# Scores of window attention: stacked 128-deep products of one head, or three 64-deep products of two heads

## The chip, the cores and the metric

The kernel runs on one core of a Trainium2 chip. The metric is device time in microseconds (us), the median of the runs. PE is the matrix engine (its weight loads are listed as PEld), DVE the vector engine, ACT the scalar engine, POOL the general engine (GpSimd), SP the queue that issues transfers.

## What is computed

One layer of a mixer for 2048 latent tokens (a grid of 32 rows by 64 columns) and 128 context tokens, 1024 channels wide, all in float32 at the inputs and outputs. One input projection feeds three branches; the change touches the third alone, attention with 8 heads of 64 channels.

```python
h = layernorm(x) * (1 + scale) + shift
xa, ba, ca, ga, u, v, gb, q, k, vv, gc = split(h @ w_in)
# latent tokens: each block of 8 x 16 queries sees its 2-D window and all 128 context keys
s_loc = q . k_window * 64**-0.5 + rel_bias      # window keys outside 8 x 16 are masked
s_ctx = q . cache_k * 64**-0.5
p = softmax(concat[s_loc, s_ctx]);  out = p_loc @ v_window + p_ctx @ cache_v
# context tokens: dense attention among the 128 context tokens
y = concat[conv branch, gMLP branch, out * silu(gc)] @ w_out
x_new = layernorm(ALPHA * x + gate * y) * ln_g + ln_b
```

## The kernel before

Activations lie with channels in the partitions, split into a float16 high and low part (`h_hi`, `h_lo`), and so are the weights. After a stage for the gMLP branch and the values, a list of jobs is worked off: for each head pair `hp` (0 to 3) a job `q`, a job `k` and a job `gc`, with jobs of the convolution (`xa`, `ca`, `ba`, `ga`) between them. A job makes 128 output channels for the five token tiles of `TILES` (four of 512, one of 128), 24 matmuls a tile, in `proj` (L505). The last stage is the output projection.

For each head pair, the `q` job (L1186) rounds the projected queries into `QS`: for head h, float16 high parts in one half of the partitions and the rest (low parts) in the other half, by two ACT and two DVE instructions a tile on 64 partitions each. The `k` job (L1195) writes the keys' high parts `KH` and low parts `KL`, each head in its own half, and SP then copies each half of `KH` and `KL` into the other half of the head's plane (L1223 to L1227). So a matmul over 128 partitions gives high times key plus low times key at once, and the scores of a head are two products: with `KH` and with `KL`.

Attention of a head pair is 17 units: 16 blocks of 128 queries (window keys: 352 columns in the first four units, 480 in the next eight, 384 in the last four, and 128 context keys each) and the 128 context queries. `scores(u, h)` (L993) issues the four matmuls of one head of a unit (two for unit 16) into a tile `s` of PSUM, of which there are two buffers, and the start of the softmax: DVE adds the bias table `TB` and takes the row's maximum (L1020, "reduce" below; it frees `s`, and the bias table for POOL to build the next one, L979) and scales the maximum (L1025). The rest of the softmax follows as five events: `expo` (L1029, ACT), `norm` (L1032 and L1033, DVE), `high` (L1036, ACT), `low` (L1039, DVE) and `turn` (L1045, a transposing transfer on SP). `values` (L1053) multiplies the turned probabilities `ptr` with the values, two heads in the two column halves of the array, and DVE writes the gated result (L1072, `yc`).

What stands where in each engine's row is decided when the program is built. A planned clock `now` advances by the columns of each projection matmul over 2.4 GHz (`tick`), by the score columns in `scores` and by 240 ns a block of keys in `values`; events are posted with a due time on that clock and come out between two projection matmuls when they are due. The table `T` holds the times: a unit of a head pair every `pace` (6.0, 6.0, 4.9 and 4.7 us), the second head half a pace after the first, and the five events 0.7, 0.7, 2.1, 2.75 and 3.7 us after the scores of their head. Each engine then works strictly through its row and waits where an operand is missing. The next `q` job drains what is left of the attention of the pair before (`finish`, L1243).

Of the kernel before, what the change touches and what calls it, by code (L numbers as in the profile page):

```python
# [22 lines left out]
P = 128  # L23
D = 1024
KB = 8
LAT = 2048
CTX = 128
TOK = LAT + CTX
# [57 lines left out]
    a_half=0.5,  # L86
    pace=(6000.0, 6000.0, 4900.0, 4700.0),
# [48 lines left out]
def hybrid_step(ctx: ExitStack, tc: tile.TileContext, x_prompt, x_sample, cache_k, cache_v, c, c_ctx,  # L136
# [781 lines left out]
    QS = ap.tile([P, 2, TOK], F16, name="QS")  # L918
    KH = ap.tile([P, 2, TOK + CTX], F16, name="KH")
    KL = ap.tile([P, 2, TOK + CTX], F16, name="KL")  # L920
# [61 lines left out]
    class Attn:  # L982
        def __init__(self, hp, pace):
            self.hp = hp
            self.ys = None
            self.ts = {}
            for u in range(17):
                if u:
                    post(T['a_start'][hp] + (u - T['a_tab']) * pace, lambda u=u: make_tables(u), ("at", hp, u))
                for h in range(2):  # L990
                    post(T['a_start'][hp] + (u + T['a_half'] * h) * pace, lambda u=u, h=h: self.scores(u, h), ("as", hp, u))

        def scores(self, u, h):  # L993
            i = 2 * u + h
            drain(("a", self.hp, i - T['a_guard']), ("at", self.hp, u))
            tg = ("a", self.hp, i)
            sm = ap.tile([P, 4], F32, name="sm", bufs=8)
            s = aps.tile([P, 2, 512], F32, name="s", tag="s", bufs=2)
            if u < 16:
                rb, j = UNITS[u]  # L1000
                nr = RB_NROW[rb]
                n = 32 * nr
                q = QS[:, h, u * P:(u + 1) * P]
                for e, kk in enumerate((KH, KL)):
                    PE.matmul(out=s[:, 0, 384:512], lhsT=q, rhs=kk[:, h, TOK:TOK + CTX], start=(e == 0), stop=(e == 1))
                for e, kk in enumerate((KH, KL)):
                    win = kk[:, h, RB_ROW0[rb] * 64:(RB_ROW0[rb] + nr) * 64].rearrange("p (r c) -> p r c", c=64)
                    PE.matmul(out=s[:, 1, 0:n], lhsT=q, rhs=win[:, :, COL0[j]:COL0[j] + 32], start=(e == 0), stop=(e == 1))  # L1008
            else:
                n = 0  # L1010
                q = QS[:, h, LAT:TOK]
                for e, kk in enumerate((KH, KL)):
                    PE.matmul(out=s[:, 0, 384:512], lhsT=q, rhs=kk[:, h, LAT:TOK], start=(e == 0), stop=(e == 1))
            now[0] += 2 * (P + n) / 2.4
# [113 lines left out]
    while cidx < len(jobs):  # L1128
# [37 lines left out]
        for ti, (t0, n) in enumerate(TILES):  # L1166
# [19 lines left out]
            if kind == "q":  # L1186
                for u in range(4 * ti, min(4 * ti + 4, 17)):
                    drain(("as", idx - 1, u))
                S.activation(out=QS[0:64, 0, t0:t0 + n], in_=ps[0:64], func=AF.Copy, scale=cq[0:64])
                S.activation(out=QS[64:128, 1, t0:t0 + n], in_=ps[64:128], func=AF.Copy, scale=cq[64:128])  # L1190
                V.scalar_tensor_tensor(out=QS[64:128, 0, t0:t0 + n], in0=ps[0:64], scalar=cq[0:64],
                                       in1=QS[0:64, 0, t0:t0 + n], op0=ALU.mult, op1=ALU.subtract)
                V.scalar_tensor_tensor(out=QS[0:64, 1, t0:t0 + n], in0=ps[64:128], scalar=cq[64:128],
                                       in1=QS[64:128, 1, t0:t0 + n], op0=ALU.mult, op1=ALU.subtract)
            elif kind == "k":  # L1195
                for h in range(2):
                    a = slice(64 * h, 64 * h + 64)
                    S.activation(out=KH[a, h, t0:t0 + n], in_=ps[a], func=AF.Copy, scale=ckk[a])  # L1198
                    V.scalar_tensor_tensor(out=KL[a, h, t0:t0 + n], in0=ps[a], scalar=ckk[a], in1=KH[a, h, t0:t0 + n],  # L1199
                                           op0=ALU.mult, op1=ALU.subtract)  # L1200
                rng = {1: (0, 1024), 3: (1024, 2048)}.get(ti)
                if ti == 0:
                    cps = aps.tile([P, P], F32, name="cps", tag="o")
                    PE.transpose(cps, ckt, ident)
                    for h in range(2):
                        a = slice(64 * h, 64 * h + 64)
                        S.activation(out=KH[a, h, TOK:], in_=cps[a], func=AF.Copy, scale=s_k[a])
                        V.scalar_tensor_tensor(out=KL[a, h, TOK:], in0=cps[a], scalar=s_k[a], in1=KH[a, h, TOK:],
                                               op0=ALU.mult, op1=ALU.subtract)
                if ti == 4:  # L1210
                    rng = (2048, TOK + CTX)
# [155 lines left out]
```

## Time and profile before

| | before |
|---|---|
| runs | 1193.34, 1196.65, 1197.59 us (median 1196.65) |
| profiled execution | 1199.64 us, span 1197.7 us |
| PE busy | 1070.1 us (89%) |
| DVE busy | 846.7 us (71%) |
| ACT busy | 444.8 us (37%) |
| POOL busy | 346.2 us (29%) |
| granted clock of PE | 0.963 of 2.4 GHz over the span |
| attention of head pair 0, 1, 2, 3 | from 423, 565, 712, 840 to some 533, 678, 806, 940 us |

A busy time is a sum over the span, so the shares say which engine could be the bound, and the windows of the four attention stretches say in which of them it is. In a timeline the first column is the start, the second the duration; matmuls overlap in the array, so what one costs there is the distance between two starts. A wait belongs to the instruction that waited, and the arrow names what ended it. Between the four stretches lie the `k` jobs (some 30 us each), in which no attention runs.

### The profile page before, as it was taken

What the parts mean: (1) busy time and instruction counts of PE and PEld (TensorE: products, weight loads), DVE (VectorE), ACT (ScalarE), POOL (GpSimd) and SP (SyncE); (2) the same over time, 40 slices, a digit from 0 to 9 for tenths busy, and PEclk for the clock granted to TensorE, in tenths of its full rate; (3) what the DMA queues carried; (4) which work ended last, traced back from release to release, by engine and by line L of the source; (5) the groups of instructions that cost most, each with busy time, mean ns of one, the idle gap of its engine ahead of it and who ended that gap; (6) DMA issues with size and microseconds to landing.
All of it is one profiled execution on the core that took longest, in us unless ns stands there. A gap on an engine that the chain in (4) does not pass through costs nothing. (4 is left out here: it accounts for less than half of the span.)

```text
span 1197.7 us, 21038 instructions
## 1 busy us (share of the span) xinstructions
PE 1070.1 (89%) x8044; PEld 684.0 (57%) x8044; DVE 846.7 (71%) x2073; ACT 444.8 (37%) x756; POOL 346.2 (29%) x346
## 2 busy tenths in 40 slices
PE   5378989889986999999999999989988999888885
PEld 1267875468773555554545445545545477776674
DVE  1778875665662379863898549983899558877877
ACT  0233322122322356543655436663666321112111
POOL 0135765200002032101662022300325405434434
PEclk9589999889997999999999999999999999999998
DMA  9703201348969237755566646767466663343341
GB/s 346 238 5 113 85 9 56 130 153 292 295 206 245 52 80 134 143 112 122 101 143 130 144 103 131 150 121 157 94 139 117 203 200 108 124 139 105 111 136 53
DMA packets 254356, 165.50 MB, mean 138 GB/s; under 512 B 163600, under 2 KB 224808, under 8 KB 254256
## 3 DMA queue, kind: packets, MB, share of 16 engines
q1 hardware_dynamic: 254256, 164.16, 52.7%
q8 instruction: 63, 1.03, 0.4%
q14 instruction: 37, 0.30, 0.1%
HBM read 88.06 MB, written 36.21 MB: 104 GB/s over the span
## 5 line engine op out<-in xcount | busy, mean ns | idle before, releaser
L508 PE MATMUL pj<-h_hi,wring 128*128 128x512 f16 (+1 forms) x1280 | 335.9, 349 | 9.6 <-DMA wring<-wj_d 9.6
L508 PEld LDWEIGHTS <-wring 128*128 128x128 f16 x2400 | 212.9, 99 | 224.6 <-DMA wring<-wj_d 9.7
L508 PE MATMUL pj<-h_lo,wring 128*128 128x512 f16 (+1 forms) x640 | 217.7, 349 | 0.0
L1296 PE MATMUL ps<-wo,yh 128*128 128x512 f32 (+1 forms) x840 | 193.6, 390 | 20.9 <-DVE yh L1106 20.9
L1296 PEld LDWEIGHTS ps<-wo,yh 128*128 128x128 f32 x840 | 154.0, 189 | 60.4 <-DVE yh L1106 27.0
L1039 DVE SCALAR_TENSOR_TENSOR PH<-pt,sm,PH 128x608 f16<-128x608 f32 (+3 forms) x136 | 155.6, 1144 | 2.6 <-ACT PH L1036 2.4
L979 POOL TENSOR_TENSOR TB<-raw,msk 128x480 f32<-128x480 f32 (+2 forms) x96 | 96.1, 1010 | 186.9 <-DVE sm L1020 186.8
L1036 ACT ACTIVATE PH<-pt,sm 128x608 f16<-128x608 f32 (+3 forms) x136 | 99.9, 734 | 95.1 <-ACT pt L1029 63.3
L1029 ACT ACTIVATE pt<-pt,sm,scal 128x608 f32<-128x608 f32 (+2 forms) x128 | 108.3, 846 | 56.9 <-DVE sm L1025 53.3
L1020 DVE CUSTOM_DVE_ANT_0 pt<-s,TB 128x608 f32<-128x608 f32 (+2 forms) x128 | 93.3, 729 | 10.5 <-PE s L1008 9.7
L518 PE MATMUL vvps<-wV,h_hi 128*128 128x256 f16 x544 | 92.9, 275 | 3.7 <-DVE vt L900 3.6
L518 PEld LDWEIGHTS <-h_hi 128*128 128x128 f16 x816 | 80.8, 100 | 20.3 <-issue 9.3
L508 PE MATMUL p<-h_hi,wring 128*128 128x512 f16 (+1 forms) x320 | 87.2, 358 | 2.9 <-DVE th L525 2.9
L1320 ACT ACTIVATE r<-r,omv 128x1024 f32<-128x1024 f32 x16 | 19.9, 1245 | 177.2 <-issue 141.1
L508 PEld LDWEIGHTS <-wB 128*128 128x128 f16 x768 | 65.9, 102 | 25.6 <-issue 3.4
L1321 POOL TENSOR_TENSOR r<-r,gam 128x1024 f32<-128x1024 f32 x16 | 38.2, 2387 | 128.0 <-ACT r L1320 128.0
L518 PE MATMUL vvps<-wV,h_lo 128*128 128x256 f16 x272 | 74.8, 275 | 0.0
L508 PE MATMUL ups<-h_hi,wB 128*128 128x128 f16 (+2 forms) x448 | 72.9, 274 | 0.0
L963 POOL TENSOR_SCALAR raw<-raw,scal 128x528 f32<-128x528 f32 x8 | 5.5, 704 | 219.8 <-DVE scal L189 165.4
L1106 DVE TENSOR_TENSOR yh<-yf,yh 128x1024 fp32r<-128x1024 f32 x17 | 41.0, 2410 | 35.2 <-ACT yh L1105 35.2
L1199 DVE SCALAR_TENSOR_TENSOR KL<-pj,scal,KH 64x512 f16<-64x512 f32 (+1 forms) x40 | 26.8, 669 | 54.1 <-ACT KH L1198 53.9
L456 POOL TENSOR_TENSOR h_lo<-hf,h_hi 128x512 f16<-128x512 f32 x34 | 39.9, 1179 | 85.0 <-DMA wstage<-in_w_in_dram 37.8
(212 smaller groups left out, 1715.4 us busy)
## 6 DMA issues: line engine op xcount, KB each, us to landing
wa<-in_w_ada_dram SPq DMA_DIRECT2D x24, 512.0 KB, 7.2
wraw<-in_w_in_dram SPq DMA_DIRECT2D x20, 512.0 KB, 5.7
wj_d<-wsp SPq DMA_DIRECT2D x40, 256.0 KB, 6.1
wring<-wj_d SPq DMA_DIRECT2D x20, 512.0 KB, 6.0
yf<-y_d SPq DMA_DIRECT2D x17, 512.0 KB, 5.6
xt<-in_x_sample_dram SPq DMA_DIRECT2D x16, 512.0 KB, 4.7
VW<-v_d SPq DMA_DIRECT2D x64, 128.0 KB, 5.1
xr<-in_x_sample_dram SPq DMA_DIRECT2D x16, 512.0 KB, 4.1
```

What stands on the lines that cost most here:

```text
L456: G.tensor_tensor(out=h_lo[:, k0:k0 + g, t0:t0 + n], in0=hv, in1=hi, op=ALU.subtract)
L508: PE.matmul(out=ps, lhsT=w(a, k) if callable(w) else w[:, a, k, :], rhs=mov(b, k), start=(k == 0 and i == 0), stop=(k == KB - 1 and i == 2))
L518: PE.matmul(out=ps, lhsT=a[:, k, i * P:(i + 1) * P], rhs=w[:, b, k, :], start=(k == 0 and q == 0), stop=(k == KB - 1 and q == 2))
L979: G.tensor_tensor(out=TB[:, tslot(u) + h, P:P + n], in0=raws[h][:, off:off + n], in1=msk[:, mo:mo + n], op=ALU.add)
L1020: V.tensor_tensor_reduce(out=pt[:, :w], in0=src, in1=TB[:, tslot(u) + h, 0:w], op0=ALU.add, op1=ALU.max, scale=1.0, scalar=-3e38, accum_ou ...
L1029: S.activation(out=pt[:, :w], in_=src, func=AF.Exp, bias=sm[:, 1:2], scale=st_["isig"], accum_out=sm[:, 2:3])
L1036: S.activation(out=pb[:, 0:w], in_=pt[:, :w], func=AF.Copy, scale=sm[:, 3:4])
L1039: V.scalar_tensor_tensor(out=pb[:, wp:wp + w], in0=pt[:, :w], scalar=sm[:, 3:4], in1=pb[:, 0:w], op0=ALU.mult, op1=ALU.subtract)
L1106: V.tensor_tensor(out=yh[:, 1], in0=yf, in1=yh[:, 0].bitcast(F32), op=ALU.subtract)
L1199: V.scalar_tensor_tensor(out=KL[a, h, t0:t0 + n], in0=ps[a], scalar=ckk[a], in1=KH[a, h, t0:t0 + n], op0=ALU.mult, op1=ALU.subtract)
L1296: PE.matmul(out=ps, lhsT=yh[:, a, k, :], rhs=wo[:, b, k, f0:f1], start=(k == 0 and q == 0), stop=(k == KB - 1 and q == 2))
L1321: G.tensor_tensor(out=r, in0=r, in1=gam, op=ALU.mult)
```

## The change

`QH`, `QL`, `KH` and `KL` hold the queries' and keys' high and low parts with the channels where the projection leaves them: head 0 in partitions 0 to 63, head 1 in 64 to 127. One ACT and one DVE instruction on 128 partitions write a tile, and the 24 copies by SP are gone. The scores of a head are now three products over 64 partitions (high with high, low with high, high with low; the fourth, low with low, is left out), 12 matmuls a unit in which the two heads alternate. `scores(u)` issues both heads of a unit; the softmax's start is in a function of its own, `soft(u, h)`, which is posted for the second head half a pace later, as before. The planned clock advances by 3 times the columns of a unit instead of 4 times. Nothing in `T` is changed.

```diff
             for u in range(17):
                 if u:
                     post(T['a_start'][hp] + (u - T['a_tab']) * pace, lambda u=u: make_tables(u), ("at", hp, u))
+                post(T['a_start'][hp] + u * pace, lambda u=u: self.scores(u), ("as", hp, u))
                 for h in range(2):
-                    post(T['a_start'][hp] + (u + T['a_half'] * h) * pace, lambda u=u, h=h: self.scores(u, h), ("as", hp, u))
+                    post(T['a_start'][hp] + (u + T['a_half'] * h) * pace, lambda u=u, h=h: self.soft(u, h), ("as", hp, u))
...
-        def scores(self, u, h):
-            i = 2 * u + h
-            drain(("a", self.hp, i - T['a_guard']), ("at", self.hp, u))
+        def scores(self, u):
+            drain(("a", self.hp, 2 * u - T['a_guard']), ("at", self.hp, u))
...
+            s = [aps.tile([P, 2, 512], F32, name="s", tag="s", bufs=2) for h in range(2)]
+            pairs = ((QH, KH), (QL, KH), (QH, KL))
+            for e, (q, kk) in enumerate(pairs):
+                for h in range(2):
+                    a = slice(64 * h, 64 * h + 64)
+                    k0 = TOK if u < 16 else LAT
+                    PE.matmul(out=s[h][:, 0, 384:512], lhsT=q[a, t0:t0 + P], rhs=kk[a, k0:k0 + CTX], start=(e == 0), stop=(e == 2))
...
-            now[0] += 2 * (P + n) / 2.4
+            now[0] += 3 * (P + n) / 2.4
+            self.ss[u] = s
+
+        def soft(self, u, h):
+            i = 2 * u + h
+            tg = ("a", self.hp, i)
+            sm = ap.tile([P, 4], F32, name="sm", bufs=8)
+            s = self.ss[u][h]
...
-                S.activation(out=QS[0:64, 0, t0:t0 + n], in_=ps[0:64], func=AF.Copy, scale=cq[0:64])
-                S.activation(out=QS[64:128, 1, t0:t0 + n], in_=ps[64:128], func=AF.Copy, scale=cq[64:128])
-                V.scalar_tensor_tensor(out=QS[64:128, 0, t0:t0 + n], in0=ps[0:64], scalar=cq[0:64],
...
+                S.activation(out=QH[:, t0:t0 + n], in_=ps, func=AF.Copy, scale=cq)
+                V.scalar_tensor_tensor(out=QL[:, t0:t0 + n], in0=ps, scalar=cq, in1=QH[:, t0:t0 + n],
+                                       op0=ALU.mult, op1=ALU.subtract)
...
-                if rng:
-                    r = slice(*rng)
-                    for kk in (KH, KL):
-                        SP.dma_start(out=kk[64:128, 0, r], in_=kk[0:64, 0, r])
-                        SP.dma_start(out=kk[0:64, 1, r], in_=kk[64:128, 1, r])
```

In PE's row, a unit of 480 window columns of head pair 0. Before, one head (the other stands half a pace later, behind more projection matmuls):

```order
L1005 LDWEIGHTS QS_4034
L1005 MATMUL s_4917<-KH_4035,QS_4034 128x128
L1005 LDWEIGHTS QS_4034
L1005 MATMUL s_4917<-KL_4036,QS_4034 128x128
L1008 LDWEIGHTS QS_4034
L1008 MATMUL s_4917<-KH_4035,QS_4034 128x480
L1008 LDWEIGHTS QS_4034
L1008 MATMUL s_4917<-KL_4036,QS_4034 128x480
L508 LDWEIGHTS wring_4130
```

Now the second half of the unit's 12 matmuls (both heads, `s_4915` and `s_4916`):

```order
L1016 LDWEIGHTS QH_4034
L1016 MATMUL s_4915<-KH_4036,QH_4034 128x480
L1016 LDWEIGHTS QH_4034
L1016 MATMUL s_4916<-KH_4036,QH_4034 128x480
L1016 LDWEIGHTS QL_4035
L1016 MATMUL s_4915<-KH_4036,QL_4035 128x480
L1016 LDWEIGHTS QL_4035
L1016 MATMUL s_4916<-KH_4036,QL_4035 128x480
L1016 LDWEIGHTS QH_4034
L1016 MATMUL s_4915<-KL_4037,QH_4034 128x480
L1016 LDWEIGHTS QH_4034
L1016 MATMUL s_4916<-KL_4037,QH_4034 128x480
```

Both heads stand together, once a unit. Over the whole row PE goes from 128-deep, 128-wide matmuls to the two-headed ones of `values` or of the scores, or between those two, 263 times; before it was 136 times (`values` alone). Behind the last `values` of head pair 3, 980 matmuls are left; before it was 997.

In DVE's row, one unit (480 window columns) of head pair 0, from its first reduce (L1020 before, L1032 now) to its last instruction ahead of the next unit. Before (`sm_5003` and `pt_5009` are head 0, `sm_5058` is head 1, `pt_4978` is head 1 of the unit before):

```order
L1020 ISA pt_5009,sm_5003<-s_5004,TB_4039 128x608
L1020 ISA sm_5003 128x1
L1025 TENSOR_SCALAR sm_5003<-sm_5003,scal_85 128x1
L1039 SCALAR_TENSOR_TENSOR PH_4040<-pt_4978,sm_4972,PH_4040 128x608
L1032 TENSOR_SCALAR sm_5003<-sm_5003 128x1
L1033 RECIPROCAL sm_5003<-sm_5003 128x1
L1072 SCALAR_TENSOR_TENSOR yc_4960<-o_5025,scal_85,sgc_4038 128x8x16
L1020 ISA pt_5064,sm_5058<-s_5059,TB_4039 128x608
L1020 ISA sm_5058 128x1
L1025 TENSOR_SCALAR sm_5058<-sm_5058,scal_85 128x1
L1039 SCALAR_TENSOR_TENSOR PH_4040<-pt_5009,sm_5003,PH_4040 128x608
L1032 TENSOR_SCALAR sm_5058<-sm_5058 128x1
```

Now (`sm_5021` is head 0, `sm_5067` head 1; L1044 and L1045 are `norm`, L1051 is `low`, L1084 is `yc`):

```order
L1037 TENSOR_SCALAR sm_5021<-sm_5021,scal_85 128x1
L1044 TENSOR_SCALAR sm_5021<-sm_5021 128x1
L1045 RECIPROCAL sm_5021<-sm_5021 128x1
L1084 SCALAR_TENSOR_TENSOR yc_4964<-o_5035,scal_85,sgc_4039 128x8x16
L1032 ISA pt_5068,sm_5067<-s_5008,TB_4040 128x608
L1032 ISA sm_5067 128x1
L1037 TENSOR_SCALAR sm_5067<-sm_5067,scal_85 128x1
L1051 SCALAR_TENSOR_TENSOR PH_4041<-pt_5022,sm_5021,PH_4041 128x608
L1044 TENSOR_SCALAR sm_5067<-sm_5067 128x1
L1045 RECIPROCAL sm_5067<-sm_5067 128x1
L1051 SCALAR_TENSOR_TENSOR PH_4041<-pt_5068,sm_5067,PH_4041 128x608
```

Before, the `low` of the head ahead stands between a head's reduce and its `norm`. Now nothing but at times a `yc` stands between reduce and `norm` of head 0, and the `low` of head 1 stands right behind the `norm` of head 1, ahead of the next unit's reduce.

In DVE's row, a unit of head pair 3 now, its second head (`sm_10431`; before, the row had the order shown above in this place too, with the `low` ahead of the `norm`):

```order
L1032 ISA pt_10432,sm_10431<-s_10400,TB_4040 128x608
L1032 ISA sm_10431 128x1
L1037 TENSOR_SCALAR sm_10431<-sm_10431,scal_85 128x1
L1084 SCALAR_TENSOR_TENSOR yc_10383<-o_10436,scal_85,sgc_4039 128x8x16
L1044 TENSOR_SCALAR sm_10431<-sm_10431 128x1
L1045 RECIPROCAL sm_10431<-sm_10431 128x1
L1051 SCALAR_TENSOR_TENSOR PH_4041<-pt_10414,sm_10413,PH_4041 128x608
```

The `norm` of head 1 now stands ahead of the `low` of head 0; head 0 of the same unit has its rows in the order of before. Head pair 2 reads the same way; in head pair 1 most units kept the order of before.

## Rows read from the trace of the kernel before

**Rows 1.** The windows view: the four attention stretches (head pairs 0 to 3) and the units with 480 window columns of head pair 0; columns: the stretch in us, its length, busy us (and instructions) of PE, PEld, DVE, ACT and POOL, the granted clock of PE, the share of the transfer engines, GB/s.

```profile
423.00:533.00 110.00, 109.17 (x984) 58.91 (x982) 91.55 (x238) 64.45 (x117) 20.68 (x21) 1.00 0.62 117
565.00:678.00 113.00, 110.67 (x978) 59.69 (x977) 95.06 (x250) 64.01 (x117) 47.22 (x47) 0.98 0.61 123
712.00:806.00 94.00, 88.04 (x850) 48.28 (x849) 84.47 (x232) 64.24 (x118) 22.19 (x23) 1.00 0.67 129
840.00:940.00 100.00, 91.30 (x868) 49.97 (x867) 89.16 (x234) 58.27 (x107) 37.67 (x37) 0.98 0.61 116
...
454.00:495.00 41.00, 41.00 (x401) 22.36 (x400) 37.70 (x92) 26.42 (x45) 10.13 (x10) 1.00 0.79 142
```

**Rows 2.** The waits view for PE, one row each from the stretches of head pairs 0, 1 and 3 and then two of head pair 2: who waited for whom, us in total, times, longest.

```profile
PE o L1064 <- DMA ptr<-PH: 0.8, 1, 0.8
...
PE o L1064 <- DMA ptr<-PH: 2.3, 1, 2.3
...
PE o L1064 <- DMA ptr<-PH: 8.7, 10, 1.4
...
PE o L1064 <- DMA ptr<-PH: 4.8, 5, 1.7
...
PE s L1005 <- DVE sm L1020: 0.3, 1, 0.3
```

**Rows 3.** The timeline of PE in head pair 0: the four score matmuls of one head (480 window columns) and the projection matmul behind them.

```profile
459.22 0.22 PE L1005 MATMUL s<-KH,QS 128*128 128x128 f16 x1
459.28 0.22 PE L1005 MATMUL s<-KL,QS 128*128 128x128 f16 x1
459.33 0.37 PE L1008 MATMUL s<-KH,QS 128*128 128x480 f16 x1
459.54 0.37 PE L1008 MATMUL s<-KL,QS 128*128 128x480 f16 x1
459.74 0.59 PE L508 MATMUL pj<-h_hi,wring 128*128 128x512 f16 x2
```

**Rows 4.** The timeline of PE at the first `values` of head pair 0: 24 matmuls of 64 columns of weights, the two heads in the two column halves, between two projection matmuls.

```profile
435.88 0.38 PE L508 MATMUL pj<-h_lo,wring 128*128 128x512 f16 x1
436.19 0.36 PE L1064 MATMUL o<-ptr,v_ctx 128*64 128x128 f16 x6
436.38 0.67 PE L1064 MATMUL o<-ptr,VW 128*64 128x128 f16 x18
436.98 0.39 PE L508 MATMUL pj<-h_hi,wring 128*128 128x512 f16 x1
```

**Rows 5.** The timeline of PE in the gMLP stage: a matmul that is one row deep (L208) between 256-column matmuls over all 128 rows.

```profile
177.24 0.27 PE L518 MATMUL vps<-wB,h_lo 128*128 128x256 f16 x1
177.44 0.38 PE L208 MATMUL ax<-scal,ones 1*128 1x1 f32 x2
177.75 0.28 PE L518 MATMUL vps<-wB,h_hi 128*128 128x256 f16 x1
```

**Rows 6.** The timelines of DVE, then POOL, then ACT over one head of a 480-column unit of head pair 2, with a table build on POOL.

```profile
750.20 0.79 DVE L1020 CUSTOM_DVE_ANT_0 pt<-s,TB 128x608 f32<-128x608 f32 x1
...
751.03 0.21 DVE L1025 TENSOR_SCALAR sm<-sm,scal 128x1 f32<-128x1 f32 x1
751.17 1.65 DVE L1039 SCALAR_TENSOR_TENSOR PH<-pt,sm,PH 128x608 f16<-128x608 f32 x1
752.74 0.14 DVE L1032 TENSOR_SCALAR sm<-sm 128x1 f32<-128x1 f32 x1
...
753.04 0.79 DVE L1020 CUSTOM_DVE_ANT_0 pt<-s,TB 128x608 f32<-128x608 f32 x1
...
751.08 1.09 POOL L979 TENSOR_TENSOR TB<-raw,msk 128x480 f32<-128x480 f32 x1 [1.75 <-DVE sm L1020]
...
751.28 0.89 ACT L1029 ACTIVATE pt<-pt,sm,scal 128x608 f32<-128x608 f32 x1 [0.15 <-DVE sm L1025]
752.09 0.18 ACT L1029 ACTIVATION_READ_ACCUMULATOR pt<-pt,sm,scal 128x1 f32 x1
753.16 0.80 ACT L1036 ACTIVATE PH<-pt,sm 128x608 f16<-128x608 f32 x1 [0.89 <-ACT pt L1029]
```

**Rows 7.** The timeline of DVE over one head of a 480-column unit of head pair 2 without a table build on POOL.

```profile
739.68 0.79 DVE L1020 CUSTOM_DVE_ANT_0 pt<-s,TB 128x608 f32<-128x608 f32 x1
...
740.65 0.85 DVE L1039 SCALAR_TENSOR_TENSOR PH<-pt,sm,PH 128x608 f16<-128x608 f32 x1
741.79 0.15 DVE L1032 TENSOR_SCALAR sm<-sm 128x1 f32<-128x1 f32 x1 [0.29 <-ACT pt L1029]
...
742.09 0.79 DVE L1020 CUSTOM_DVE_ANT_0 pt<-s,TB 128x608 f32<-128x608 f32 x1
```

**Rows 8.** The groups of instructions by line, shapes apart, over the four attention stretches: a query tile's second DVE instruction (count, busy us, mean ns, idle before); then, from the timeline of DVE in head pair 2, a query tile's first DVE instruction with its wait.

```profile
L1193 DVE SCALAR_TENSOR_TENSOR QS<-pj,scal,QS 64x512 f16<-64x512 f32 x12 | 9.1, 755 | 0.2
...
799.65 0.74 DVE L1191 SCALAR_TENSOR_TENSOR QS<-pj,scal,QS 64x512 f16<-64x512 f32 x1 [1.05 <-ACT QS L1190]
```

**Rows 9.** The timelines of PE and of DVE in head pair 1: the scores of head 0 of unit 9 start, and the reduce of head 1 of unit 8.

```profile
618.60 0.22 PE L1005 MATMUL s<-KH,QS 128*128 128x128 f16 x1
...
619.50 0.78 DVE L1020 CUSTOM_DVE_ANT_0 pt<-s,TB 128x608 f32<-128x608 f32 x1
```

**Rows 10.** The DMA view: the copies between the halves of `KH` and of `KL`, KB each, us from issue to landing.

```profile
KH<-KH SPq DMA_DIRECT2D x16, 128.0 KB, 2.2
```

More of the change, by code (lines that the diff above doesn't have):

```diff
@@ L917, in hybrid_step @@
     pg, aps = open_pool("aps", bufs=1, space=PSUM)
-    QS = ap.tile([P, 2, TOK], F16, name="QS")
-    KH = ap.tile([P, 2, TOK + CTX], F16, name="KH")
-    KL = ap.tile([P, 2, TOK + CTX], F16, name="KL")
+    QH = ap.tile([P, TOK], F16, name="QH")
+    QL = ap.tile([P, TOK], F16, name="QL")
+    KH = ap.tile([P, TOK + CTX], F16, name="KH")
+    KL = ap.tile([P, TOK + CTX], F16, name="KL")
     VW = ap.tile([P, 8, 4, 256], F16, name="VW")
@@ L986, in __init__ @@
             self.ts = {}
+            self.ss = {}
             for u in range(17):
@@ L1002, in scores @@
                 n = 32 * nr
[L1003 to L1013, printed above, removed]
-            now[0] += 2 * (P + n) / 2.4
+            t0 = u * P
+            s = [aps.tile([P, 2, 512], F32, name="s", tag="s", bufs=2) for h in range(2)]
[5 more added lines that the diff above has]
+                    PE.matmul(out=s[h][:, 0, 384:512], lhsT=q[a, t0:t0 + P], rhs=kk[a, k0:k0 + CTX], start=(e == 0), stop=(e == 2))
+            if u < 16:
+                for e, (q, kk) in enumerate(pairs):
+                    for h in range(2):
+                        a = slice(64 * h, 64 * h + 64)
+                        win = kk[a, RB_ROW0[rb] * 64:(RB_ROW0[rb] + nr) * 64].rearrange("p (r c) -> p r c", c=64)
+                        PE.matmul(out=s[h][:, 1, 0:n], lhsT=q[a, t0:t0 + P], rhs=win[:, :, COL0[j]:COL0[j] + 32],
+                                  start=(e == 0), stop=(e == 2))
+            now[0] += 3 * (P + n) / 2.4
[5 more added lines that the diff above has]
+            s = self.ss[u][h]
+            n = 32 * RB_NROW[UNITS[u][0]] if u < 16 else 0
             w = P + n
@@ L1188, in hybrid_step @@
                     drain(("as", idx - 1, u))
[L1189 to L1201 removed]
+                S.activation(out=QH[:, t0:t0 + n], in_=ps, func=AF.Copy, scale=cq)
+                V.scalar_tensor_tensor(out=QL[:, t0:t0 + n], in0=ps, scalar=cq, in1=QH[:, t0:t0 + n],
+                                       op0=ALU.mult, op1=ALU.subtract)
+            elif kind == "k":
+                S.activation(out=KH[:, t0:t0 + n], in_=ps, func=AF.Copy, scale=ckk)
+                V.scalar_tensor_tensor(out=KL[:, t0:t0 + n], in0=ps, scalar=ckk, in1=KH[:, t0:t0 + n],
+                                       op0=ALU.mult, op1=ALU.subtract)
                 if ti == 0:
@@ L1204, in hybrid_step @@
                     PE.transpose(cps, ckt, ident)
[L1205 to L1209, printed above, removed]
+                    S.activation(out=KH[:, TOK:], in_=cps, func=AF.Copy, scale=s_k)
+                    V.scalar_tensor_tensor(out=KL[:, TOK:], in0=cps, scalar=s_k, in1=KH[:, TOK:],
+                                           op0=ALU.mult, op1=ALU.subtract)
                 if ti == 4:
-                    rng = (2048, TOK + CTX)
                     kp = tmpA.tile([P, P], F32, name="kp", tag="th")
```

4 lines of the change are left out of this document (1 added, 3 removed).

## The prediction

> **What bounds the kernel now.** I read the windows of the four attention stretches first, then the waits of PE in them, then single instructions in the timelines. The profiled execution took 1199.64 us (span 1197.7), 3.0 more than the median of the three runs, 1196.65; what I add up is a difference, and I put it on the median. A measurement of this kernel tells some 0.5%, 6 us, from no change.
>
> In all four stretches the clock is near full and PE is busy nearly all the time [rows 1], but that busy time does not make PE the bound in all of them. In the stretch of head pair 0 it waits 0.8 us in all, in that of pair 1 2.3 us; in pair 3 it waits ten times and 8.7 us for turned probabilities, in pair 2 five times and 4.8 us, and there it once waits for a reduce too [rows 2]. The probabilities come late because DVE is late: it is busy for 84 of 94 and 89 of 100 us there [rows 1], and where one looks closely it has no pause from one reduce to the next [rows 6]. So pairs 0 and 1 are bound by PE with DVE close behind (37.7 of 41 us in the widest units of pair 0 [rows 1]), pairs 2 and 3 by DVE.
>
> **The scores on PE.** The two products of one head with 128 + 480 columns take 459.74 - 459.22 = 0.52 us, 0.428 ns a column [rows 3]. A head pair has 8,960 such columns a product (4 x 480 + 8 x 608 + 4 x 512 + 128), and four products of them before: 15.3 us. Afterwards there are six, in three pairs that lie in the two row halves. No row shows two row halves at work. The nearest are the two column halves of `values`: 24 matmuls of 128 columns in 436.98 - 436.19 = 0.79 us [rows 4], so 12 pairs of 66 ns at most, against 55 for one such matmul alone [rows 3]; if leaving that shape costs what entering it costs (next sentence), a pair takes 58. Entering it costs 436.19 - 435.88 = 0.31 us where the 512 columns alone take 0.22, so 0.09; ahead of a matmul that is one row deep, 0.20 instead of 0.11 for 256 columns, again 0.09 [rows 4, 5]. I take that for row halves, in and out. Pairs at 3 ns over one matmul make 3 x 8,960 x 0.428 + 99 x 3 ns = 11.8 us, a gain of 3.5 us a head pair. The shape changes 127 times more often in the whole row, 32 a head pair: 2.9 us. PE's own work thus falls by 0.6 us a head pair. The other end is pairs that do not overlap: six products, 23.0 us, so PE's work rises by 7.7 + 2.9 = 10.6 us. I take the lower end, since both sorts of halves are halves of one array and the columns' rows are the nearest.
>
> The Trainium skill (TensorE: Matmul & The Clock Gate, LDWEIGHTS) says that loading weights takes the columns over 1.2 GHz, however few rows they have, which is 107 ns for 128 columns, so that a pair would need 213 ns for its two loads. This trace differs: 128-column matmuls, each with a load of its own, start 55 ns apart [rows 3].
>
> **The plan's clock.** It counts 3 instead of 4 products, so a head pair's 17 units hold 8,960 / 2.4 = 3.7 us more projection. In pair 3 this shows as 17 matmuls fewer behind the last `values` (980 instead of 997), 17 x 0.219 = 3.7 us. That is gained where PE had been waiting anyway, in pair 3. In pairs 0 to 2 the next `q` job ends the stretch after the same projections, and nothing is gained by it.
>
> **The order on DVE.** Here I see the main cost. Before, DVE does the `low` of the head ahead while ACT does `expo`, then `norm`: a head takes 753.04 - 750.20 = 2.84 us with a table build on POOL, and 742.09 - 739.68 = 2.41 us without [rows 6, 7]. The build starts as the reduce ends, and the `low` beside it takes 1.65 us instead of 0.85 [rows 6, 7], so a wait in its place is partly free.
>
> In pairs 2 and 3 the second head's `norm` now stands ahead of the `low`. Counted from a reduce: the scaled maximum is there after 1.04 us, `expo` runs from 1.08 to 2.07 (its second row ends at 752.27), `norm` may start at 2.10 and takes 0.30 (752.74 to 753.04) [rows 6]; then the `low`, with the build over (752.17), 0.85: 3.25 us. That is 0.41 more than 2.84 with a build and 0.84 more than 2.41 without. Three units of four are followed by a build (units with j = 2 share a table), so 0.52 us a unit; over 14 of the 17 units, leaving the first and the narrow last ones out, 7.3 us a head pair. From below the cost is nothing, if other work of DVE's row always falls into the pause; from above it is 17 x 0.84 = 14 us.
>
> In pair 0 the first head has reduce and `norm` with no `low` between: 2.40 us. The second has reduce, `low` and `norm`, 2.84 with a build, and then its own `low`, which waits for `high`: that starts 0.12 after `norm` and takes 0.80 [rows 6], then 0.85. The unit takes 2.40 + 2.84 + 0.92 + 0.85 = 7.0 us with a build, 6.6 without, some 6.9 in the mean, where it took 5.7 before. PE's unit there is the pace of 6.0 us, and 6.1 with the 2% by which a matmul takes longer than planned. The eight widest units fall behind by 0.8 us each, 6.4 us; DVE may lag by some 1.7 us before PE has to wait (next part), so PE waits 4.7 us. The wait of 0.8 us that is there now is taken up in it: +3.9, and with PE's -0.6, +3.3 us. The narrower units need about 6 us on DVE, and I count nothing for them.
>
> In pair 1 most units keep the order of before, and I set the few that don't against what the queries save below.
>
> **One pair of score tiles.** Both heads' scores now wait until the second head's reduce of the unit before is done; before, that reduce had half a pace more. In pair 0 it ends 2.40 + 0.83 = 3.2 us after the unit's first reduce, and PE comes to the next scores some 6.1 - 1.2 = 4.9 us after that (1.0 us of scores, 0.2 until DVE has them), hence the 1.7 us. In pair 1, head 0 of unit 9 starts at 618.60 while the reduce of unit 8's second head ends at 620.29 [rows 9]: PE will wait 1.7 us there, and behind it stand all projections. After that DVE's lag is shorter by as much, so I count it once: with the -0.6, +1.1 us for pair 1. In pairs 2 and 3 PE waits for DVE anyway. DVE doesn't starve by it: from that reduce to the next stand 2 us of its work, while the scores take 0.2 + 0.6 + 0.2 us.
>
> **Queries and keys.** A query tile gets one DVE instruction less, 0.755 us, and its first no longer waits behind two on ACT, about half of the 1.05 us that DVE waits for ACT [rows 8]. Three such tiles fall into the stretch of pair 2 after DVE is late: 3 x 1.25 = 3.8 us. The keys' share of it falls into the `k` jobs, where DVE has pauses, and counts nothing. Nor do the copies on SP: they land in 2.2 us [rows 10], the attention starts 5.7 us or more after the `k` job, and no row of PE's waits names them.
>
> **The sum.** Pair 0 +3.3; pair 1 +1.1; pair 2 +7.3 - 3.8 = +3.5; pair 3 +7.3 - 3.7 = +3.6. Together +11.5 us: 1211.1 for the profiled execution, 1208.2 on the median.
>
> **The rivals.**
>
> *DVE hides the new waits, and it gets faster.* If rows of the jobs (`sgc`, `z`, `yc`) fall into the pauses and the `low` that no longer meets a build gives the rest back, the cost of the order is nothing and no reduce comes late: -0.6 for pair 0, -0.6 for pair 1, -3.8 and -3.7, together -8.7 us, 1188. For it speaks that 0.41 us is little, and that a `low` beside a build takes twice its time; against it that DVE waits 0.29 us for `expo` even now, with the `low` ahead, wherever no build slows the `low` [rows 7]. I give it 0.18.
>
> *Half of it.* With the order at half its price and the gains whole, pair 0 gives 2.4 - 0.8 - 0.6 = +1.0, pair 1 +1.1, pair 2 3.7 - 3.8 and pair 3 3.7 - 3.7: +2 us, 1199, no change. 0.16.
>
> *The halves don't run together.* PE's work rises by 10.6 us a pair: pairs 0 and 1 by that much; in pair 2 88.0 + 10.6 us of work against DVE's 97.5, +4.6; in pair 3 91.3 + 10.6 + 3.7 = 105.6 against 107.3, so +3.6 as in the forecast. Together +29: 1226. Against it stand the column halves [rows 4]. 0.10.
>
> *The weights hold the pairs.* If the two loads of a pair come one after the other at the 55 ns of rows 3, a pair of 128 columns takes 110 instead of 58, and 17 x 3 x 52 ns = 2.7 us are added in each pair, of which PE shows those of pair 1 and part of those of pair 0: some +15, 1212. 0.06; it lies in the forecast's range. The skill's load time, in the section named, is the rule that speaks for it; by it such a pair would take 213 ns.
>
> **How the numbers follow.** The forecast has 0.50, its own range 1202 to 1217. With the two other slower cases, and a little of the forecast's lower edge taken off, slower by over 0.5% has 0.64; faster has 0.18, and within 0.5% 0.18. The range from 1188 to 1222 leaves out about half of the first rival and the third.
>
> **What would show it.** In the changed kernel's profile the starts of the two heads' score matmuls should lie a few ns apart and pairs of 480 columns some 0.21 us, with 0.09 us more at either end of the twelve. In pair 3, DVE's `norm` of each second head should wait some 0.8 us for ACT, and in pair 0 the second head's `low` 0.9 us for `high`; the stretch of pair 3 should be some 7 us longer, that of pair 0 some 4. PE should wait for reduces at the first score matmul, where it hardly did. I am wrong if DVE's waits for ACT hardly grow, if PE's starts within the twelve lie a full matmul apart, or if the clock falls in the new waits of PE.

## The result and the profile after

| | before | after |
|---|---|---|
| runs | 1193.34 to 1198.68 us, median 1197.12 of 4 | 1210.11 to 1215.99 us, median 1211.06 of 4 |
| profiled execution | 1199.64 us, span 1197.7 | 1211.67 us, span 1209.9 |
| ratio of the times | | 1.0124, 95% interval 1.0102 to 1.0146 |

Slower, as forecast: 1208.2 was predicted, and 1211.06 is inside the range. The stretches below go from the transpose of a pair's key tile on PE (L1220 after, first start 421.80) to the next pair's L1210 (549.01), for pair 3 to the first matmul of the output stage; each length is a difference of two starts in PE's timeline.

| stretch, us | pair 0 | pair 1 | pair 2 | pair 3 | rest of the span |
|---|---|---|---|---|---|
| before | 120.8 | 125.4 | 105.3 | 131.7 | 714.6 |
| after | 127.2 | 123.6 | 106.8 | 136.0 | 716.3 |
| difference (predicted) | +6.4 (+3.3) | -1.8 (+1.1) | +1.5 (+3.5) | +4.4 (+3.6) | +1.7 (0) |

The sum of 12.2 agrees with the 11.5 predicted, but the places don't: pair 0 lost twice what I gave it, pair 1 gained.

Each stretch is read from one execution, and the granted clock of PE is not the same in all of them. Before, it was at 1.2 GHz from 625.3 to 628.7 in pair 1, right behind a wait of PE of 2.3 us, and from 918.8 to 922.2 and from 966.6 to 970.0 in pair 3. After, it was at 2.4 GHz through all of pairs 0 to 2 and fell once in pair 3, from 978.8 to 982.2, in the last wait below. In 3.4 us at half the clock PE loses up to 1.7, so the clock alone can account for most of pair 1's -1.8: that the change gains there is not shown.

The group of `low` on the page of before, then the page of the kernel after: engines over the span, and the groups of `low` and of the keys' rounding.

```profile
L1039 DVE SCALAR_TENSOR_TENSOR PH<-pt,sm,PH 128x608 f16<-128x608 f32 (+3 forms) x136 | 155.6, 1144 | 2.6 <-ACT PH L1036 2.4
...
PE 1071.8 (89%) x8308; PEld 667.0 (55%) x8308; DVE 794.1 (66%) x2029; ACT 417.7 (35%) x712; POOL 345.2 (29%) x346
...
L1051 DVE SCALAR_TENSOR_TENSOR PH<-pt,sm,PH 128x608 f16<-128x608 f32 (+3 forms) x136 | 134.5, 989 | 16.5 <-ACT PH L1048 16.4
...
L1206 DVE SCALAR_TENSOR_TENSOR KL<-pj,scal,KH 128x512 f16<-128x512 f32 (+1 forms) x20 | 13.4, 671 | 69.7 <-ACT KH L1205 69.7
```

DVE does less work than before (846.7 us then), and yet the kernel is slower: the `low` now waits 16.4 us for `high`, where it waited 2.4.

PE's wait at the end of pair 3 before, then its waits after: from the stretches of pairs 0 and 1, two rows of pair 2 and two of pair 3.

```profile
PE p L508 <- DVE th L525: 2.9, 1, 2.9
...
PE s L1010 <- DVE sm L1032: 5.2, 8, 1.5
...
PE s L1010 <- DVE sm L1032: 3.3, 3, 1.8
...
PE s L1010 <- DVE sm L1032: 4.1, 8, 0.7
PE o L1076 <- DMA ptr<-PH: 1.4, 2, 0.8
...
PE s L1010 <- DVE sm L1032: 10.9, 12, 1.6
PE p L508 <- DVE cvt L1184: 5.2, 1, 5.2
```

PE's waits have moved from the turned probabilities at `values` [rows 2] to the reduces at the first score matmul, as the prediction said they would. The wait at the end of pair 3, for the last tiles of the convolution's jobs, has grown from 2.9 to 5.2 us.

DVE's waits for ACT: `norm` before in pairs 0, 2 and 3; then after, two rows of pair 0, and `norm` in pairs 2 and 3.

```profile
DVE sm L1032 <- ACT pt L1029: 3.9, 11, 0.9
...
DVE sm L1032 <- ACT pt L1029: 2.4, 6, 0.9
...
DVE sm L1032 <- ACT pt L1029: 2.7, 5, 0.9
...
DVE sm L1044 <- ACT pt L1041: 15.2, 21, 1.1
DVE PH L1051 <- ACT PH L1048: 12.4, 17, 0.9
...
DVE sm L1044 <- ACT pt L1041: 14.7, 21, 0.9
...
DVE sm L1044 <- ACT pt L1041: 14.9, 23, 0.9
```

Over the four stretches DVE waits 69.9 us for ACT at `norm` and `low`, and before it waited 17.4 (the waits view adds up waits of over 0.2 us).

The timeline of DVE in one 480-column unit of pair 0 after, from the first head's reduce to that of the next unit.

```profile
471.93 0.78 DVE L1032 CUSTOM_DVE_ANT_0 pt<-s,TB 128x608 f32<-128x608 f32 x1
...
474.03 0.15 DVE L1044 TENSOR_SCALAR sm<-sm 128x1 f32<-128x1 f32 x1 [1.05 <-ACT pt L1041]
...
474.54 0.78 DVE L1032 CUSTOM_DVE_ANT_0 pt<-s,TB 128x608 f32<-128x608 f32 x1
...
475.50 1.66 DVE L1051 SCALAR_TENSOR_TENSOR PH<-pt,sm,PH 128x608 f16<-128x608 f32 x1
477.08 0.14 DVE L1044 TENSOR_SCALAR sm<-sm 128x1 f32<-128x1 f32 x1
...
478.34 0.85 DVE L1051 SCALAR_TENSOR_TENSOR PH<-pt,sm,PH 128x608 f16<-128x608 f32 x1 [0.92 <-ACT PH L1048]
479.11 0.79 DVE L1032 CUSTOM_DVE_ANT_0 pt<-s,TB 128x608 f32<-128x608 f32 x1
```

The first head has no `low` to fill its 1.05 us, the second head's `low` waits 0.92 us for `high`: the unit takes 479.11 - 471.93 = 7.18 us on DVE, 7.0 was predicted with a build, and PE's pace is 6.0.

The timeline of PE in pair 0 after: the twelve score matmuls of a unit with 352 window columns between two projection matmuls.

```profile
424.07 0.38 PE L508 MATMUL pj<-h_lo,wring 128*128 128x512 f16 x1
424.38 0.23 PE L1010 MATMUL s<-KH,QH 64*128 64x128 f16 x2
424.44 0.22 PE L1010 MATMUL s<-KH,QL 64*128 64x128 f16 x2
424.50 0.22 PE L1010 MATMUL s<-KL,QH 64*128 64x128 f16 x2
424.56 0.31 PE L1016 MATMUL s<-KH,QH 64*128 64x352 f16 x2
424.71 0.31 PE L1016 MATMUL s<-KH,QL 64*128 64x352 f16 x2
424.86 0.31 PE L1016 MATMUL s<-KL,QH 64*128 64x352 f16 x2
425.10 0.39 PE L508 MATMUL pj<-h_hi,wring 128*128 128x512 f16 x1
```

Each row holds a pair (x2) whose two records start 3 ns apart, and pairs of 128 columns follow each other after some 60 ns, as single matmuls did [rows 3]: the two row halves run together. Going in takes 424.38 - 424.07 = 0.31 us behind 512 columns that take 0.22 alone, and coming out 425.10 - 424.86 = 0.24 behind 352 columns that take 0.15, so 0.09 us either way, as at the column halves [rows 4]. The Trainium skill (TensorE: Matmul & The Clock Gate, Part 3: Packing small matmuls) gives about 4 ns for each further tile in the array; this trace agrees, with 3.

### The profile page after: what moved, and what is told of

It reads as the page before. It is cut to its first block, busy times and chain, and to the rows that moved or that the text cites. A ratio compares the mean times of both kernels' runs of the same rounds, so it can differ in the third digit from the quotient of the medians.

```text
span 1209.9 us, 21337 instructions
## 1 busy us (share of the span) xinstructions
PE 1071.8 (89%) x8308; PEld 667.0 (55%) x8308; DVE 794.1 (66%) x2029; ACT 417.7 (35%) x712; POOL 345.2 (29%) x346
## 5 line engine op out<-in xcount | busy, mean ns | idle before, releaser
L508 PEld LDWEIGHTS <-wring 128*128 128x128 f16 x2400 | 206.5, 99 | 239.6 <-issue 28.2
L1051 DVE SCALAR_TENSOR_TENSOR PH<-pt,sm,PH 128x608 f16<-128x608 f32 (+3 forms) x136 | 134.5, 989 | 16.5 <-ACT PH L1048 16.4
L1032 DVE CUSTOM_DVE_ANT_0 pt<-s,TB 128x608 f32<-128x608 f32 (+2 forms) x128 | 92.9, 726 | 4.2 <-PE s L1016 4.0
L1319 POOL TENSOR_TENSOR r<-r,gam 128x1024 f32<-128x1024 f32 x16 | 38.2, 2389 | 131.9 <-ACT r L1318 131.9
L1206 DVE SCALAR_TENSOR_TENSOR KL<-pj,scal,KH 128x512 f16<-128x512 f32 (+1 forms) x20 | 13.4, 671 | 69.7 <-ACT KH L1205 69.7
```

The costliest lines, as they stand in the source:

```text
L508: PE.matmul(out=ps, lhsT=w(a, k) if callable(w) else w[:, a, k, :], rhs=mov(b, k), start=(k == 0 and i == 0), stop=(k == KB - 1 and i == 2))
L1032: V.tensor_tensor_reduce(out=pt[:, :w], in0=src, in1=TB[:, tslot(u) + h, 0:w], op0=ALU.add, op1=ALU.max, scale=1.0, scalar=-3e38, accum_ou ...
L1051: V.scalar_tensor_tensor(out=pb[:, wp:wp + w], in0=pt[:, :w], scalar=sm[:, 3:4], in1=pb[:, 0:w], op0=ALU.mult, op1=ALU.subtract)
L1319: G.tensor_tensor(out=r, in0=r, in1=gam, op=ALU.mult)
```

## The experiments

Theory: the order on DVE is the cost, and DVE's lag also sets what the queries' saving is worth. Rivals: the coupled score tiles are the cost; the row halves cost more than they bring; the order matters little. The first four kernels take the parts one by one; the later ones ask where the gain of the parts that did work went.

**1. The old order back.** The planned clock goes on in the two heads' `soft` instead of at once in `scores`; the work is that of the change.

```diff
-            now[0] += 3 * (P + n) / 2.4      # in scores(u)
+            now[0] += 1.5 * (P + n) / 2.4    # in soft(u, h)
```

> The changed kernel, but the planned clock is advanced in soft (half of a unit's score columns for each head) and not in scores; DVE's row then has norm behind the low of the head ahead again. Theory (the order on DVE and ACT costs the time): the waits of DVE for ACT at norm and low fall from some 73 us over the four stretches to 20 to 30, and the time to 1185 to 1194 us. Rival A (the coupling of both heads' score tiles costs it: PE waits 24 us for reduces): those waits stay above 15 us and the time stays at 1206 to 1213. Rival B (the changes of the array's shape cost it): nothing moves, 1208 to 1213.

Measured: 1194.36 us (1191.38 to 1197.52), ratio to the kernel before 0.9984 (0.9965 to 1.0004), just above the expected 1194; DVE's waits for ACT at `norm` and `low` fall to 17.4 us, below the expected 20 to 30. DVE's row has the old order of `low` and `norm` in all four pairs, but for a unit or two; in PE's row the scores stand where they stand in the kernel after, only the `values` mostly come a few projection matmuls later, and ACT's `expo` and `high` alternate in both. The stretches are 119.5, 123.0, 102.6 and 131.9 us: against the kernel after, -7.7, -0.6, -4.1 and -4.1. So the order alone costs 16.5 us by the stretches and 16.7 by the medians, and without it the change is no slower than before, at most 0.35% faster. PE's waits here, from pair 3's stretch:

```profile
PE s L1010 <- DVE sm L1032: 6.6, 9, 1.2
PE p L508 <- DVE cvt L1184: 6.1, 1, 6.1
```

**2 and 3. The coupling alone, and the order on the kernel before.** Both have the old stacked products. In the first, both heads' scores are issued together and DVE's order stays; in the second, the clock goes on in `scores` as in the change, but by four products and not three, so DVE's order changes too, nearly as in the change.

```diff
+        def scores(self, u):                 # both heads' matmuls, both tiles s
+            ...
+            now[0] += 0 * (P + n) / 2.4      # second kernel: 4 *
+        def soft(self, u, h):                # reduce and the rest of the softmax
+            ...
+            now[0] += 2 * (P + n) / 2.4      # second kernel: 0 *
```

> The kernel before with its own four products a unit's column, but both heads' scores issued together in scores(u), the softmax posted for each head as in the changed kernel, and the planned clock advanced in soft, so that DVE's row is that of before. This is the coupling of the score tiles alone. Theory (order): a difference of at most 4 us from the kernel before, 1195 to 1201. Rival A (coupling): most of the 14 us, 1205 to 1212, with PE waiting some 20 us for reduces.

> As the one with both heads together on the products of before, but the planned clock advanced by all of a unit's score columns in scores, as the changed kernel does: DVE's row gets norm ahead of low in head pairs 0, 2 and 3. Theory (order): 12 to 20 us over the one with the order kept, 1209 to 1219. Rival A or B: the same time as that one, within 4 us.

Measured: 1197.61 us (ratio 1.001, 0.9991 to 1.0029) for the coupling alone, and 1219.84 (1.0194, 1.0158 to 1.023) with the new order, a little over the expected 1219. Coupled score tiles thus cost nothing that can be measured, within some -1 to +3.5 us. They alone move PE's waits from `values` to the reduces: in pair 3, 7.8 us for reduces and 1.3 at `values`, where before all 8.7 stood at `values`. The new order costs 22 us here: by the stretches +7.4, -0.9, +7.7 and +7.9. Pair 0 pays more than predicted (+3.9), pair 1 nothing. The other two are no test of the +7.3 predicted for each, though they are near it: by the jump of four products ACT's `expo` of the next head has also moved ahead of a `high`, in 3 units of pair 2 and 8 of pair 3, which it does nowhere in the kernel after.

**4 and 5. The queries' saving.** The query tile is rounded in two halves on ACT and two on DVE, as before the change; once in the kernel after, once with the old order back.

```diff
-                S.activation(out=QH[:, t0:t0 + n], in_=ps, ...)
-                V.scalar_tensor_tensor(out=QL[:, t0:t0 + n], in0=ps, ...)
+                for h in range(2):
+                    a = slice(64 * h, 64 * h + 64)
+                    S.activation(out=QH[a, t0:t0 + n], in_=ps[a], ...)
+                for h in range(2):
+                    a = slice(64 * h, 64 * h + 64)
+                    V.scalar_tensor_tensor(out=QL[a, t0:t0 + n], in0=ps[a], ...)
```

> The changed kernel with each query tile rounded by two ACT and two DVE instructions on 64 partitions, as before the change; all else as changed. Theory (DVE is late in head pair 2, and the queries' saving is worth 3.8 us there): 1213 to 1217 against 1211, with the stretch of head pair 2 longer by 3 to 5 us. Rival (the saving was hidden): 1209 to 1212 and that stretch within 1 us.

> The kernel with the old order on DVE back, and the queries rounded in two halves on ACT and two on DVE as before the change (five tiles a head pair, each one DVE instruction more). If that saving was worth some 13 us in the changed kernel only because DVE was late there, it is worth less with DVE's order restored: 2 to 6 us more than the kernel with the order back alone, 1196 to 1201. If it is worth the same whatever the order, 1205 to 1209.

Measured: 1225.17 us (ratio 1.0237, 1.0185 to 1.029) and 1201.0 (1.0039, 1.0017 to 1.0062), so the saving is worth 14.1 us in the kernel after and 6.6 with the old order. Both are more than I expected, the first far more: by the stretches +3.6, +2.3, +6.2 and +0.7 there, against +0.2, +1.7, +5.8 and -2.2 here. Pair 2 pays in both, but not all of it in waits: PE's waits in its stretch grow by 4.4 us in the first (from 6.5 to 10.9) and by 4.0 in the second (from 2.9 to 6.9), and then the clock falls. The second kernel's PE at that place, and the windows view behind it:

```profile
808.46 0.36 PE L1076 MATMUL o<-ptr,v_pr 128*64 128x128 f16 x6 [2.61 <-DVE yc L1084]
...
809.20:812.60 3.40, 3.40 (x24) 2.35 (x21) 0.64 (x3) 0.72 (x2) 0.00 (x0) 0.50 0.61 179
```

From 809.2 to 812.6 the granted clock is 0.50, that is 1.2 GHz, where PE loses 1.7 us; in the first kernel the same stands behind a wait of 2.9 us, from 827.5 to 830.9, and in neither kernel to compare with does the clock fall in pair 2. Waits and clock together make 6.1 and 5.7 us, which is what pair 2 pays. Pairs 0 and 1 pay where the order has made DVE late there. That part of the saving is worth something only because of the order is shown; that this part is most of it is not.

The second kernel also says what the rest of the change is worth: with the old order and without the queries' saving it is 0.39% slower than the kernel before, some 4.5 us. The clock's fall in pair 2 can be part of that; the rest stays open.

**6 and 7. Do the row halves carry the scores?** First the kernel after with all matmuls of head 0 ahead of those of head 1; then the old order with both heads' matmuls on the rows of head 0.

```diff
-            for e, (q, kk) in enumerate(pairs):
-                for h in range(2):
+            for h in range(2):
+                for e, (q, kk) in enumerate(pairs):
                     a = slice(64 * h, 64 * h + 64)   # second kernel: slice(0, 64)
```

> The changed kernel with all score products of head 0 ahead of those of head 1, so that the two row halves no longer lie beside each other in time. If the halves' overlap is what makes six products as cheap as three, the score matmuls start some 50 to 60 ns (128 columns) and 0.15 to 0.21 us (the window) apart, a head pair's scores cost PE 9 to 11 us more; where PE waits for reduces anyway (pairs 2 and 3) part of it is hidden: 1216 to 1238. If the overlap is worth nothing, the time stays at 1209 to 1214.

> The kernel with the old order on DVE back, with the second head's products taken from the rows of the first head (its scores are then those of the first head), so that both matmuls of a pair lie in the same row half and can't run together. If running together is what makes six products as cheap as three, pairs start 110 ns (128 columns) and 0.4 us (480) apart, the scores cost PE 7 to 8 us more a head pair: the stretches of pairs 0 to 2 grow by 5 to 8 us each, that of pair 3 by 0 to 4, where PE waits for reduces now, and the time is 1208 to 1222. If they are not run together even in two halves, nothing changes: 1192 to 1197.

The first gave 1213.07 us (1.0136, 1.0097 to 1.0174). That is below the 1216 to 1238 expected of an overlap that matters and inside the 1209 to 1214 of its rival, but it can't speak for the rival, because the halves still ran side by side. Its PE timeline for a unit with 352 window columns:

```profile
438.65 0.38 PE L508 MATMUL pj<-h_lo,wring 128*128 128x512 f16 x1
438.96 0.23 PE L1010 MATMUL s<-KH,QH 64*128 64x128 f16 x1
439.03 0.22 PE L1010 MATMUL s<-KH,QL 64*128 64x128 f16 x1
439.08 0.22 PE L1010 MATMUL s<-KL,QH 64*128 64x128 f16 x1
439.09 0.23 PE L1010 MATMUL s<-KH,QH 64*128 64x128 f16 x1
439.14 0.31 PE L1014 MATMUL s<-KH,QH 64*128 64x352 f16 x1
```

In PE's row the three window matmuls (L1014) of head 0 stand ahead of the second head's first matmul, yet the latter starts at 439.09, before the first L1014 at 439.14.

The second, in which the second head's scores are those of the first, gave 1228.76 us (1.0254, 1.0209 to 1.0299), above the expected 1208 to 1222. Its PE timeline for a 480-column unit:

```profile
480.00 0.28 PE L1010 MATMUL s<-KH,QH 64*128 64x128 f16 x2
480.12 0.27 PE L1010 MATMUL s<-KH,QL 64*128 64x128 f16 x2
...
480.34 0.57 PE L1016 MATMUL s<-KH,QH 64*128 64x480 f16 x2
480.75 0.57 PE L1016 MATMUL s<-KH,QL 64*128 64x480 f16 x2
```

Pairs now lie 0.11 and 0.41 us apart, twice as far. The stretches grow by 11.4, 11.2, 7.3 and 3.5 us over the old order's: PE's scores take 11.4 us more in pair 0 (from start to start), where the prediction had 23.0 - 11.8 = 11.2 for it. The expectation was too low because I took there the 7.7 us that stand against the four products of before. With the old order, running together is worth 34 us of this kernel.

**8. Is moving projections into the stretches a gain?** The planned clock counts four products, so that the projections stand among the units as before the change.

```diff
-            now[0] += 3 * (P + n) / 2.4      # in scores(u)
+            now[0] += 2 * (P + n) / 2.4      # in soft(u, h)
```

> The changed kernel with a planned clock that counts four of the six products, so that the projections lie among the units as in the kernel before, and DVE's order is that of before too. If the projections that the change's clock moves forward in pair 3 are given back in a wait for the w_out splits, the stretch of pair 3 is within 1 us of the one with the clock at three products, PE's wait for cvt falls from 6 to about 3 us, and the time is 1192 to 1197. If moving them is a gain, pair 3 is 3.7 us longer: 1197 to 1200.

Measured: 1194.15 us (1189.33 to 1199.8; 0.9978, 0.9956 to 1.0001), the same as with three products. PE's wait at the end of pair 3 is 1.0 us (for `th`, L525) instead of 6.1. So the 3.7 us were not a gain in the time. The stretch of pair 3 is 4.5 us shorter, not within 1 us, in a profiled execution that was the fastest of twelve (1189.33). PE's waits in it are 3.4 us shorter in all, and the clock stays at 2.4 GHz to its end, where in experiment 1 it fell to 1.2 GHz from 959.1 to 966.0, in and behind the wait of 6.1 us.

**9 to 11. What holds the end of pair 3.** In experiment 1's timelines PE runs dry at 953.7 and goes on at 960.04. DVE's and ACT's rows hold the last `th` and `cvt` behind the splits of `w_out`, and these wait for transfers. ACT there:

```profile
946.84 1.06 ACT L1134 ACTIVATE wo<-wos 128x1024 fp32r<-128x1024 f32 x1 [0.93 <-DMA wos<-in_w_out_dram]
949.19 1.06 ACT L1134 ACTIVATE wo<-wos 128x1024 fp32r<-128x1024 f32 x1 [1.30 <-DMA wos<-in_w_out_dram]
950.16 0.67 ACT L524 ACTIVATE th<-p,scal 128x512 f32<-128x512 f32 x1
951.46 1.06 ACT L1134 ACTIVATE wo<-wos 128x1024 fp32r<-128x1024 f32 x1 [0.63 <-DMA wos<-in_w_out_dram]
955.26 1.06 ACT L1134 ACTIVATE wo<-wos 128x1024 fp32r<-128x1024 f32 x1 [2.75 <-DMA wos<-in_w_out_dram]
957.01 1.06 ACT L1117 ACTIVATE yh<-yf 128x1024 fp32r<-128x1024 f32 x1 [0.70 <-DMA yf<-y_d]
957.98 0.67 ACT L524 ACTIVATE th<-p,scal 128x512 f32<-128x512 f32 x1
```

The eight pieces go through three staging tiles, and their issues stand on SP behind the last attention result. Three kernels follow, all on experiment 1: the attention planned some 3 us earlier; four staging tiles; and both together, with the first split of `y` posted 1.5 us later.

```diff
-    a_start=(7400.0, 6000.0, 5650.0, 6200.0),
+    a_start=(4400.0, 3400.0, 3200.0, 3200.0),        # kernels 1 and 3
...
-            outp[k] = outp["op"].tile([P, D], F32, name="wos", bufs=3)
+            outp[k] = outp["op"].tile([P, D], F32, name="wos", bufs=4)   # 2 and 3
...
-    out_split=3100.0,
+    out_split=4600.0,                                # kernel 3
```

> The kernel with the old order on DVE back (the planned clock goes on by half of the scores' six products), and the attention stretches planned to start some 2.5 to 3 us earlier, since the key copies on SP that they left room for are gone. If the projections at the end of pair 3 wait for the splits of w_out because PE is there too early, more of them lie behind the last values and the time is 1186 to 1192. If the time is held by the amount of work on PE and DVE alone, it is as without the earlier start: 1192 to 1197.

> The kernel with the old order on DVE back, and four staging tiles for w_out instead of three. If PE's wait of 6 us for cvt or th at the end of pair 3 is set by the eight w_out pieces, whose transfers start behind the last attention result on SP's queue and go round three buffers, the wait falls by 2 to 4 us, to 2 to 4, and the time to 1190 to 1193. If the wait is set by DVE's and ACT's own row (the splits' 1.06 and 1.23 us each), it stays at 5 to 7 us and the time at 1192 to 1197.

> The earlier start of the attention, four staging tiles, and the first split of y planned 1.5 us later so that one more th stands ahead of it. If the three act on the same chain, PE's wait at the end of pair 3 falls from 6.2 to 1 to 4 us and the time is 1187 to 1192. If the chain is bound elsewhere, 1192 to 1196, as with the earlier start alone.

The earlier start gave 1193.65 us (0.997, 0.995 to 0.999): no different from experiment 1, above the expected 1186 to 1192, and PE's last wait stayed at 6.2 us. It leaves 994 matmuls behind the last `values`, where experiment 1 leaves 980 and experiment 8, with its wait of 1.0 us, 997: how many are left does not by itself say how long PE waits. The first piece of `w_out` goes out at 935.9 here and at 934.8 in experiment 1, though the last attention result is there 2.7 us earlier. Four staging tiles gave 1191.55 (0.9958, 0.9937 to 0.998), as expected, though that interval overlaps experiment 1's, and the wait fell from 6.1 to 3.4 us:

```profile
PE p L508 <- DVE cvt L1184: 3.4, 1, 3.4
```

All together gave 1187.78 us (0.9929, 0.9896 to 0.9962), with waits of 3.0 and 0.6 us, again as expected. So the wait at the end of pair 3 hangs in part on `w_out`'s round of staging tiles; what the later split of `y` adds was not tried by itself. This version is faster than the kernel before by 0.7% and than the changed one by some 2%; how much of it the staging tiles would give to the kernel before was not tried.

## Why the prediction was right, and where it was off

**The sum.** The forecast has 18.5 us for the order on DVE (3.9 + 7.3 + 7.3) and -7.0 for everything else. By the medians the order cost 16.7 (1211.06 against 1194.36), and everything else gave -2.4 (1194.36 against 1196.76). So the main mechanism and its size were right. That the total came within 3 us is partly luck, since the terms below miss in both directions.

**The bound** was read rightly: DVE set the pace where it was late. It was spared 52.6 us of work (846.7 to 794.1) and waited 52.5 us longer for ACT.

**Scores on PE.** -0.6 us a head pair was predicted. The stretch of pair 0 is the test: without its 0.8 us of waiting it took 120.8 - 0.8 = 120.0 before, and with the old order, where PE doesn't wait, 119.5. So -0.5: the halves' overlap and the 0.09 us a shape change were both right. The rivals "the halves don't run together" and "the weights hold the pairs" fall.

**The order on DVE** was the right mechanism, and it alone makes the kernel slower. By experiment 1 it costs 7.7, 0.6, 4.1 and 4.1 us, where 3.9, 0, 7.3 and 7.3 were predicted. In pair 0 (+4.7 of waits less 0.8) I let only the eight widest units fall behind, "the narrower units need about 6 us on DVE, and I count nothing for them". But the `low` waits 17 times for `high` in that pair, 12.4 us in all, once in each unit; in the narrower units the first heads' reduces lie 6.5 us apart in the mean, and in the wide ones 7.0, as predicted. So DVE is late when the wide units begin, and four of PE's eight waits for reduces lie in the narrow units behind them (1.9 of the 5.2 us). PE's waits in the pair are 5.9 us; the other 1.8 of the 7.7 stand in no wait that the view shows and stay open. In pairs 2 and 3 the term was too large: in pair 2's wide units the reduces of the first heads lie 5.96 us apart instead of 5.68 with a build, and 5.53 instead of 4.78 without, so some 0.3 and 0.75 a unit where 0.41 and 0.84 were predicted. Over 14 units that makes some 5.5 us; why the stretch shows only 4.1 is open.

**One pair of score tiles** (+1.7 in pair 1) fails: the wait that I read off is there, 3.3 us for reduces in pair 1, but in place of the 3.7 us at `values` that its stretch held before, not on top of them. Experiment 2 has the same: 1.6 for reduces and 2.0 at `values`, 3.6 in all. Its time alone, uncertain by some 2 us, could not exclude 1.7.

**Queries and keys.** -3.8 us was too small; 6.6 to 14 were measured. "Three such tiles fall into the stretch of pair 2 after DVE is late" held for PE's waits there, 4.0 and 4.4 us; that the clock would fall behind one of them, for another 1.7, is not in the forecast. The step that failed is that pairs 0 and 1 have nothing from it: once the order has made DVE late there, they pay 3.6 and 2.3.

**The plan's clock** (-3.7 in pair 3) fails too. Counting four products instead of three left the time the same (experiment 8), and the wait at the end of pair 3, which I had not read because my waits stopped at the last `values`, grew from 2.9 to 5.2 us. That pair 3 came out at +4.4 against +3.6 is luck: the order cost 4.1 there and not 7.3, and the clock gave nothing and not 3.7.

## What to carry to other kernels

When a planner orders several engines from one clock, a change of where that clock advances is a change of every engine's row: compare the rows first, and price each wait that now stands ahead of independent work in every unit, not only in the widest. What an engine saves is worth something only where it is late, so the worth of one edit must be read after the other edits have moved that lateness. And follow the waits past the stretch that is changed: work moved ahead of a chain that does not move with it (here transfers through a few buffers) can come back as a wait at its end. Read the granted clock of a stretch before its length is put down to an edit.

## What the runs showed of the hardware

Matmuls in the two row halves start 3 ns apart and cost one matmul, and each half runs on for itself: a matmul of the second half started 0.05 us ahead of one that stood before it in PE's row. The same matmuls in one half took 55 (128 columns) and 203 ns (480) each. Behind a wait of PE of 2.6 us the granted clock was 1.2 GHz for 3.4 us (experiment 5); after the wait of 6.1 us in experiment 1, 128-column matmuls start 0.11 us apart, and 0.06 before it. A `low` beside a table build took 1.66 us and 0.85 without one, in the kernel after as before [rows 6, 7]; as the new order takes half of them out of the builds' way, its mean fell from 1144 to 989 ns, 21 us in all, while DVE's waits for ACT grew by 52.5.
